# Attention of a four-layer kernel: one burst of products with v per chunk and tile, a table that deals the filling, and three moves in the heads

## The chip, the cores and the metric

The kernel runs on one core of a Trainium2 chip. Its time is device microseconds of one execution; lower is better. A core has TensorE (PE, the matrix engine, with a queue PEld for weight loads), VectorE (DVE), ScalarE (ACT), GpSimd (POOL) and SyncE (SP), which here only issues DMAs. Each engine works through its own list of instructions in order and waits on semaphores for the others.

## The reference

Four layers over 1024 tokens with 16 meta tokens ahead of them, model width 1024, batch 1, fp32. Layers 0 and 3 are sliding-window attention, layer 1 an mLSTM, layer 2 an HGRN2. Cut to what matters here:

```python
def attention_branch(u, w_in, q_gain, k_gain, sinks, w_out, valid, pos):
    q, k, v, z = _split(u @ w_in, (A_W, A_KVW, A_KVW, A_W))      # 16 heads of 64, 4 kv heads
    q = rope(rmsnorm(q), pos); k = rope(rmsnorm(k), pos)
    o = sliding_window_attention(q, k, v, sinks, valid)           # block 128: own and previous block
    return (o * silu(z)) @ w_out

def mlstm_branch(u, ...):
    q, k, v, ig, fg, og, z = _split(u @ w_in, B_SIZES)            # 8 heads, dk 128, dv 256
    qk = silu(causal_conv(concatenate([q, k]), conv_w, conv_b))
    h = mlstm_chunkwise(qh, kh, vh, log_i, log_f)                 # chunks of 128, running state
    h = rmsnorm(sigmoid(og) * h, h_gain)
    return (h * silu(z)) @ w_out

for i in range(4):
    h = h + branch_i(rmsnorm(h, norm_gain[i]), ...)
return h[:, meta:]
```

## The kernel before

The residual x lies transposed in SBUF: 8 tiles of 128 features by 1040 tokens. Tokens are cut in nine blocks, block 0 with the 16 meta tokens and blocks 1 to 8 of 128, and in three chunks of 400, 384 and 256 columns that hold blocks 0 to 3, 4 to 6, and 7 and 8. The last layer leaves the meta tokens out.

Every large product is made of three in a rounded fp32 format: weights and activations are split in a high and a low part (wh, wl and uh, ul), and high by high, high by low and low by high are added in one accumulator. Weights come by DMA on SP's queue as `wr` (128x512), ACT writes wh, VectorE wl (L188, L189). The norm of a layer's input, chunk by chunk, gives uh (ACT) and ul (VectorE). `proj` (L233) multiplies weights by 400, 384 or 256 columns of u; `proj_v` (L279) multiplies u, as weights, by 256 columns of the v weights (272 in the first mLSTM head, with the gates). For block 0 `proj_v` takes `um` (L275, u's high and low part of the meta tokens side by side), which POOL copies (L392).

The order of PE's work is written out by hand. Each layer builds lists of steps `[cost, function, prefetch]`; `weave` deals a list of filling steps (projections of later tiles, gate products) between the steps of a mixer in proportion to the costs, and the list is then emitted in that order. Weights are asked for a fixed cost ahead of their first use. The scheduler sets the order of the other engines from the order in which the steps are recorded.

An attention layer has eight tiles t of two heads hh. For each tile the mixer has units: (0,), (1,) and (2,3) in the first chunk, (4,5) and (6,) in the second, (7,8) in the third; a unit is one or two blocks. Per unit and head `S_step` makes the scores (L594, L595: q as weights, high and low part of k as columns) and the softmax on VectorE and ACT, whose last operation is ACT's L623; `T_step` transposes the result on PE (L631 for block 0, L636 for block 1, L640 otherwise) and copies it, masked, to a tile Pt; `V_step` multiplies by v (L662), 64 rows of the accumulator po for each head, and after a chunk's last unit ACT copies po out (L665). At step k of the mixer stand V_step of unit k−2, T_step of unit k−1 and S_step of unit k, and the filling is dealt by a cost of 470 for each block of the unit turned.

The second layer's head is what stands ahead of its mixer: products with v of head 0 for each chunk, gates, and the first q and k projections with their convolution (L837 to L852). Its mixer needs, per head, two rows of gate values over all 128 partitions: they are written to DRAM (L808, L809) and read back by broadcast DMAs of 520 KB each (L878, L879); L899 and L895 use them. L914 is the mixer's first product with v, its weights are wd (L188).

The lists that the change touches in the heads read, before:

```python
kv = kg0[0][:2] + vg[0][::2] + kg0[0][2:] + vg[0][1::2]      # first layer: k and v of chunk 0
head = [list(vg[0][0]), list(vg[0][1]), qg[0][0] + vg[0][2]] # second layer: v of chunks 0, 1, 2
```

Here `vg[0]` of the first layer has, for blocks 0 to 3, a first and a second half in turn; `vg[0][n]` and `qg[0][n]` of the second layer are the steps of chunk n.

Of the kernel before, what the change touches and what calls it, by code (L numbers as in the profile page):

```python
# [9 lines left out]
F32 = mybir.dt.float32  # L10
F32R = mybir.dt.float32r
# [4 lines left out]
P = 128  # L16
# [19 lines left out]
LOOKAHEAD = 12000.0  # L36
TAIL_LAG = 2000.0
PRIO = 40
ROWS, TMPS, RAWS, YS, QS = 9, 5, 2, 3, 6
XS = 13  # L40
WCOLS = 1088
GAP, BURST, PAUSE = 200.0, 1300.0, 2500.0
# [67 lines left out]
def hybrid_kernel(ctx: ExitStack, tc: tile.TileContext, ins, out, layers=(0, 1, 2, 3)):  # L110
# [309 lines left out]
    def layer_a(i, j, first, last, fin):  # L420
# [40 lines left out]
        def q_split(t):  # L461


            def step(qf, n, c0, cn):
                def fn():
                    q = qf()
                    R["q", t, n] = []
                    for hh in range(2):
                        st = R["mix"].tile([P, 400], F32R, tag="qs", name=nm("qs"), bufs=QS)
                        hs, os = slice(64 * hh, 64 * hh + 64), slice(64 - 64 * hh, 128 - 64 * hh)  # L470
                        s.copy(st[hs, :cn], q[hs])
                        v.tensor_tensor(st[os, :cn], q[hs], st[hs, :cn].bitcast(F32), op=ALU.subtract)
# [95 lines left out]
        def mixer(t):  # L568
            units = []
            for n, us in enumerate((((0,), (1,), (2, 3)), ((4, 5), (6,)), ((7, 8),))):  # L570
                if last and n == 0:
                    us = us[1:]
                for k, u in enumerate(us):
                    for hh in range(2):
                        units.append(dict(t=t, n=n, unit=u, hh=hh, first=k == 0, last=k == len(us) - 1))
            return units

        def mixers():
            def S_step(w):
# [10 lines left out]
                for u, b in enumerate(unit):  # L590
                    q0 = blk(b)[0]
                    k0, kw = (0, 16 if b == 0 else 256) if b < 2 else (q0 - P, 256)
                    qb, kb = slice(q0 - c0, q0 - c0 + nq), slice(k0, k0 + kw)
                    pe.matmul(S[:nq, u, :kw], q[:, qb], kh[:, kb], start=True, stop=False)  # L594
                    pe.matmul(S[:nq, u, :kw], q[:, qb], kl[:, kb], start=False, stop=True)  # L595
# [29 lines left out]
            def T_step(w):  # L625
                unit, Sm = w["unit"], w["Sm"]
                nu = len(unit)
                pt = psum("pt", 1).rearrange("p (u q) -> p u q", u=4)
                w["Pt"] = Pt = R["mix"].tile([P, 2, 2, P], F32, tag="Pt", name=nm("Pt"), bufs=2)
                if unit[0] == 0:  # L630
                    pe.transpose(pt[:NMETA, 0, :NMETA], Sm[:NMETA, :NMETA], ident[:NMETA, :NMETA])  # L631
                    s.copy(Pt[:NMETA, 0, 0, :NMETA], pt[:NMETA, 0, :NMETA])
                    return
                if unit[0] == 1:
                    for ki, ko in enumerate((0, NMETA)):
                        pe.transpose(pt[:, ki, :], Sm[:, ko : ko + P], ident)  # L636
                    s.copy(Pt[:, 0], pt[:, :2])
                    return
                for u in range(nu):
                    pe.transpose(pt[:, u, :], Sm[:, u, :P], ident)  # L640
                turn = R["masks"][:, M_TURN : M_TURN + 258].rearrange("p (o k c) -> p o k c", o=1, k=2)[:, :, :, :P]
                both = pt.rearrange("p u (o q) -> p u o q", o=1)[:, :nu]
                v.tensor_tensor(Pt[:, :nu], both.to_broadcast([P, nu, 2, P]), turn.to_broadcast([P, nu, 2, P]),
                                op=ALU.mult)

            def V_step(ws):
                w = ws[0]
                unit, n, t = w["unit"], w["n"], w["t"]
                nq = blk(unit[0])[1]
                if w["first"]:  # L650
                    if ("o", t) not in R:
                        R["o", t] = row()
                    R["po"] = psum("po", 1)
                po = R["po"]
                c0, cn = chunks[n]
                for u, b in enumerate(unit):
                    q0 = blk(b)[0]
                    kn, kbs = (NMETA, (0,)) if b == 0 else (P, (b - 1, b))
                    for ki, kb in enumerate(kbs):
                        for hh in range(2):  # L660
                            vc = P * (t // 4) + 64 * hh
                            pe.matmul(po[64 * hh : 64 * hh + 64, q0 - c0 : q0 - c0 + nq], V[kb][:kn, vc : vc + 64],  # L662
                                      ws[hh]["Pt"][:kn, u, ki, :nq], start=(ki == 0), stop=(ki == len(kbs) - 1))
                if w["last"]:
                    s.copy(R["o", t][:, c0 : c0 + cn], po[:, :cn])  # L665
# [5 lines left out]
            def put(seg, cost, fn, w, nu):  # L671
                step = [cost * nu, hi(lambda: fn(w)), None]
                segs[seg].append(step)
                return step

            for k in range(len(pairs) + 2):
                seg = pairs[k][0]["t"] if k < len(pairs) else 8
                v2, t1, s0 = (pairs[j] if 0 <= j < len(pairs) else None for j in (k - 2, k - 1, k))
                turned = len((t1 or v2 or s0)[0]["unit"])
                if v2:  # L680
                    put(seg, 470, V_step, v2, turned)
                elif t1:
                    segs[seg].append([470 * turned, lambda: None, None])
                for hh in range(2):
                    if t1:
                        put(seg, 110, T_step, t1[hh], len(t1[hh]["unit"]))
                    if s0:
                        step = put(seg, 236, S_step, s0[hh], len(s0[hh]["unit"]))
                        if s0[hh]["last"]:
                            order["S", s0[hh]["t"], s0[hh]["n"]] = step  # L690
# [9 lines left out]

        q0, qfin0 = qg[0]
        if first:
            kv = kg0[0][:2] + vg[0][::2] + kg0[0][2:] + vg[0][1::2]
            head = [kv, spread(kg0[1] + vg[1], kfin0[0])]
            parts = [tile_of(q0[:2], qfin0[:2]), (vg[2], [])]
        else:
            head = [kg0[0] + vg[0], spread(kg0[1], kfin0[0])]
            parts = [(vg[1][:2], []), tile_of(q0[:1], qfin0[:1]), (vg[1][2:], []), tile_of(q0[1:2], qfin0[1:2])]
# [41 lines left out]
    def layer_b(i, j, fin):  # L750
# [121 lines left out]
        def mixer(h):  # L872
            W = {}

            def start():
                R["h", h, 0], R["h", h, 1] = row(), row()
                R["rb"], R["wb"] = row(), row()
                sp.dma_start(R["rb"], R["rows_d"][0, h].partition_broadcast(P))  # L878
# [637 lines left out]
```

## Time and profile before

| | |
|---|---|
| median of 3 runs | 2586.06 us (2585.69 to 2589.89) |
| profiled execution | 2588.53 us, its span 2586.7 us |
| PE busy | 2543.5 us (98%), granted clock 0.997 on average |
| VectorE busy | 1963.4 us (76%) |
| ACT busy | 1711.5 us (66%) |
| products with v, L662 | 1056 records, 77.8 to 2533.5 us |
| DMA | 126.59 MB, 49 GB/s on average |

All rows come from one profiled execution. A row of a timeline has the start and the duration in us, the engine, the line of the kernel, the operation, out<-in, the tile, and in brackets the idle time just before it with what ended it. A matmul in this format leaves two records. Ends of matmuls are modelled, so that durations overlap; what a product costs is read from the distance of starts. Line numbers are those of the kernel before; in the changed kernel they are one to eight higher (L233 becomes L234, L279 L280, L662 L667).

### The profile page before, as it was taken

What the parts mean: (1) busy time and instruction counts of PE and PEld (TensorE: products, weight loads), DVE (VectorE), ACT (ScalarE), POOL (GpSimd) and SP (SyncE); (2) the same over time, 40 slices, a digit from 0 to 9 for tenths busy, and PEclk for the clock granted to TensorE, in tenths of its full rate; (3) what the DMA queues carried; (4) which work ended last, traced back from release to release, by engine and by line L of the source; (5) the groups of instructions that cost most, each with busy time, mean ns of one, the idle gap of its engine ahead of it and who ended that gap; (6) DMA issues with size and microseconds to landing.
All of it is one profiled execution on the core that took longest, in us unless ns stands there. A gap on an engine that the chain in (4) does not pass through costs nothing.

```text
span 2586.7 us, 55774 instructions
## 1 busy us (share of the span) xinstructions
PE 2543.5 (98%) x21009; PEld 2450.1 (95%) x21009; DVE 1963.4 (76%) x5386; ACT 1711.5 (66%) x4719; POOL 145.9 (6%) x543
## 2 busy tenths in 40 slices
PE   7999999999999999999999999999999999999999
PEld 6899899989999999999999999999999999999999
DVE  7777777886767676767777788978787978777776
ACT  7768776566565656555665757878585866868872
POOL 1100110000000000000000000101000000101000
PEclk9999999999999999999999999999999999999999
DMA  4211111011111111111111101111110111211112
GB/s 139 64 36 50 50 34 52 26 59 54 46 54 46 50 48 52 42 58 42 58 34 58 54 23 50 32 37 35 34 43 26 43 63 37 63 44 49 52 39 82
DMA packets 74191, 126.59 MB, mean 49 GB/s; under 512 B 11825, under 2 KB 26033, under 8 KB 73921
## 3 DMA queue, kind: packets, MB, share of 16 engines
q1 hardware_dynamic: 73920, 123.03, 14.8%
q8 instruction: 165, 2.70, 0.4%
q14 instruction: 106, 0.86, 0.1%
HBM read 108.14 MB, written 4.26 MB: 43 GB/s over the span
## 4 chain that ended last, share of the span: by engine, by line
PE 81%; DVE 10%; ACT 7%; issue 1%; DMA 1%; POOL 0%; SPq 0%; DVEq 0%; ACTq 0%; POOLq 0%
PE pj L233 39%; PE pj L317 16%; PE pj L279 10%; PE po L662 3%; PE pm L594 1%; PE pm L595 1%; PE pt L640 1%; PE pa L514 1%; DVE t L387 1%; PE po L914 1%; DVE ul L189 1%; PE pm L886 1%; PE pm L1192 1%; PE pj L275 1%; DVE wl L189 1%
## 5 line engine op out<-in xcount | busy, mean ns | idle before, releaser
L233 PE MATMUL pj<-uh,wh 128*128 128x384 f32 (+2 forms) x2592 | 868.3, 335 | 3.0 <-ACT uh L188 3.0
L233 PE MATMUL pj<-ul,wh 128*128 128x384 f32 (+2 forms) x2592 | 833.5, 322 | 1.8 <-DVE ul L189 1.7
L233 PE MATMUL pj<-uh,wl 128*128 128x384 f32 (+2 forms) x2592 | 831.1, 321 | 0.1
L233 PEld LDWEIGHTS pj<-uh,wh 128*128 128x128 f32 x2592 | 489.6, 189 | 22.1 <-issue 11.7
L233 PEld LDWEIGHTS pj<-ul,wh 128*128 128x128 f32 x2592 | 489.5, 189 | 6.5 <-DVE ul L189 3.6
L233 PEld LDWEIGHTS pj<-uh,wl 128*128 128x128 f32 x2592 | 489.2, 189 | 0.5 <-DVE wl L189 0.4
L189 DVE TENSOR_TENSOR wl<-wr,wh 128x512 fp32r<-128x512 f32 (+1 forms) x338 | 229.5, 685 | 54.2 <-ACT wh L188 49.3
L320 DVE TENSOR_TENSOR x<-x,pj 128x384 f32<-128x384 f32 (+2 forms) x480 | 235.6, 509 | 44.7 <-PE pj L317 42.6
L279 PE MATMUL pj<-wh,uh 128*128 128x256 f32 (+1 forms) x896 | 259.2, 289 | 0.7 <-ACT uh L188 0.7
L188 ACT CAST wh<-wr 128x512 fp32r<-128x512 f32 (+1 forms) x338 | 203.3, 613 | 83.1 <-PE pj L317 30.6
L279 PE MATMUL pj<-wh,ul 128*128 128x256 f32 (+1 forms) x896 | 253.5, 283 | 0.7 <-DVE ul L189 0.7
L317 PE MATMUL pj<-yh,wh 128*128 128x384 f32 (+2 forms) x768 | 253.0, 329 | 0.0
L279 PE MATMUL pj<-wl,uh 128*128 128x256 f32 (+1 forms) x896 | 252.7, 282 | 0.0
L317 PE MATMUL pj<-yl,wh 128*128 128x384 f32 (+2 forms) x768 | 247.4, 322 | 3.1 <-DVE yl L189 3.1
L317 PE MATMUL pj<-yh,wl 128*128 128x384 f32 (+2 forms) x768 | 246.8, 321 | 0.0
L279 PEld LDWEIGHTS pj<-wh,uh 128*128 128x128 f32 x896 | 169.4, 189 | 1.8 <-ACT uh L188 0.9
L408 ACT ACTIVATE t<-t 128x384 f32<-128x384 f32 (+2 forms) x240 | 117.7, 490 | 80.5 <-DVE t L407 77.8
L279 PEld LDWEIGHTS pj<-wh,ul 128*128 128x128 f32 x896 | 169.5, 189 | 1.2 <-DVE ul L189 1.1
L279 PEld LDWEIGHTS pj<-wl,uh 128*128 128x128 f32 x896 | 169.5, 189 | 0.7
L188 ACT CAST yh<-r 128x400 fp32r<-128x400 f32 (+2 forms) x144 | 68.6, 477 | 144.4 <-PE pj L317 134.8
L407 DVE SCALAR_TENSOR_TENSOR t<-pj,t 128x384 f32<-128x384 f32 (+2 forms) x192 | 98.8, 514 | 70.2 <-ACT t L406 66.4
L317 PEld LDWEIGHTS pj<-yl,wh 128*128 128x128 f32 x768 | 144.9, 189 | 5.0 <-DVE yl L189 4.7
(269 smaller groups left out, 5377.1 us busy)
## 6 DMA issues: line engine op xcount, KB each, us to landing
wr<-in_b_win SPq DMA_DIRECT2D x128, 256.0 KB, 2.7
wr<-in_a_win SPq DMA_DIRECT2D x80, 256.0 KB, 2.8
wr<-in_c_win SPq DMA_DIRECT2D x64, 256.0 KB, 2.7
r<-rowsd SPq DMA_DIRECT2D x16, 520.0 KB, 5.0
wr<-in_a_wout SPq DMA_DIRECT2D x32, 256.0 KB, 2.8
wr<-in_b_wout SPq DMA_DIRECT2D x32, 256.0 KB, 2.6
t<-t SPq DMA_DIRECT2D x96, 48.0 KB, 1.9
wr<-in_c_wout SPq DMA_DIRECT2D x16, 256.0 KB, 2.8
```

The costliest lines, as they stand in the source:

```text
L188: s.copy(h, src)
L189: v.tensor_tensor(l, src, h.bitcast(F32), op=ALU.subtract)
L233: pe.matmul(acc[:, :cn], a[:, k, :], b[:, k, c0 : c0 + cn], start=(k == 0 and i == 0), stop=(k == KT - 1 and i == 2))
L275: pe.matmul(acc[:48, :width], um[:, k, :], m[:, kk, :], start=(k == 0 and m is wh), stop=(k == KT - 1 and m is wl))
L279: pe.matmul(acc[:cn, :width], a[:, k, c0 : c0 + cn], m[:, kk, :], start=(k == 0 and i == 0), stop=(k == KT - 1 and i == 2))
L317: pe.matmul(acc[:, :cn], a[:, k, mc], b, start=(k == 0 and i == 0), stop=(k == 1 and i == 2))
L320: v.tensor_tensor(x[:, m, c0 : c0 + cn], x[:, m, c0 : c0 + cn], acc[:, :cn], op=ALU.add)
L387: v.scalar_tensor_tensor(u, x[:, k, cs], ngain[:, self.i, k : k + 1], self.acc[n], op0=ALU.mult, op1=ALU.mult)
L407: v.scalar_tensor_tensor(a[:, :cn], z, 0.0, a[:, :cn], op0=ALU.min, op1=ALU.subtract)
L408: s.activation(a[:, :cn], a[:, :cn], AF.Exp)
L514: pe.matmul(st[:, 2 * k : 2 * k + 2], sq[:, z : z + P], R["masks"][:, 0:P:64], start=True, stop=True)
L662: pe.matmul(po[64 * hh : 64 * hh + 64, q0 - c0 : q0 - c0 + nq], V[kb][:kn, vc : vc + 64], ws[hh]["Pt"][:kn, u, ki, :nq], start=(ki == 0), ...
```

## The change

1. `V_step` takes all units of a chunk and tile at once (`group`), after the last of them is turned, and copies the accumulator at its end.
2. So all Pt of a chunk have to live until then: block 0's has a small tile of its own (`Pt0`), single units of head 1 have `Pt1`, those of head 0 borrow a v tile, and units of two blocks keep `Pt`. The q tiles get two sizes, which makes room.
3. The filling is dealt by `SPACE`, a cost per unit, instead of 470 per block of the unit turned.
4. Block 0's scores are made over 128 columns of q instead of its 16; only the 16 are read.
5. The first layer's head makes block 0's v after that of blocks 1 to 3, in both halves.
6. The second layer's head has the first part of the q projection ahead of chunk 1's products with v instead of ahead of chunk 2's.
7. The two broadcast rows of mLSTM head 0 are asked for on POOL's queue; the other heads stay on SP's.

```diff
+SPACE = {(0,): 300.0, (1,): 470.0, (2, 3): 940.0, (4, 5): 870.0, (6,): 900.0, (7, 8): 940.0}
...
-                        st = R["mix"].tile([P, 400], F32R, tag="qs", name=nm("qs"), bufs=QS)
+                        w = 256 if n == 2 else 400
+                        st = R["mix"].tile([P, w], F32R, tag=f"qs{w}", name=nm("qs"), bufs=2 if n == 2 else 4)
...
-                    qb, kb = slice(q0 - c0, q0 - c0 + nq), slice(k0, k0 + kw)
-                    pe.matmul(S[:nq, u, :kw], q[:, qb], kh[:, kb], start=True, stop=False)
+                    qb, kb = slice(q0 - c0, q0 - c0 + P), slice(k0, k0 + kw)
+                    pe.matmul(S[:, u, :kw], q[:, qb], kh[:, kb], start=True, stop=False)
...
+                if nu == 2:
+                    Pt = R["mix"].tile([P, 512], F32, tag="Pt", name=nm("Pt"), bufs=2)
+                elif w["hh"]:
+                    Pt = R["mix"].tile([P, 256], F32, tag="Pt1", name=nm("Pt"), bufs=1)
+                else:
+                    Pt = vtile()[:, :256]
...
-            def V_step(ws):
+            def V_step(group):
...
-                for u, b in enumerate(unit):
-                    q0 = blk(b)[0]
+                for ws, u, b in ((ws, u, b) for ws in group for u, b in enumerate(ws[0]["unit"])):
+                    q0, nq = blk(b)
...
-                if w["last"]:
-                    s.copy(R["o", t][:, c0 : c0 + cn], po[:, :cn])
+                s.copy(R["o", t][:, c0 : c0 + cn], po[:, :cn])
...
-                if v2:
-                    put(seg, 470, V_step, v2, turned)
-                elif t1:
-                    segs[seg].append([470 * turned, lambda: None, None])
+                group += [v2] if v2 else []
+                space = SPACE[(t1 or v2 or s0)[0]["unit"]]
+                if v2 and v2[0]["last"]:
+                    put(seg, space, V_step, group, 1)
+                    group = []
+                elif t1 or v2:
+                    segs[seg].append([space, lambda: None, None])
...
-            kv = kg0[0][:2] + vg[0][::2] + kg0[0][2:] + vg[0][1::2]
+            kv = kg0[0][:2] + vg[0][2::2] + vg[0][:1] + kg0[0][2:] + vg[0][3::2] + vg[0][1:2]
...
-                sp.dma_start(R["rb"], R["rows_d"][0, h].partition_broadcast(P))
-                sp.dma_start(R["wb"], R["rows_d"][1, h].partition_broadcast(P))
+                queue = sp if h else g
+                queue.dma_start(R["rb"], R["rows_d"][0, h].partition_broadcast(P))
+                queue.dma_start(R["wb"], R["rows_d"][1, h].partition_broadcast(P))
...
-        head = [list(vg[0][0]), list(vg[0][1]), qg[0][0] + vg[0][2]]
+        head = [vg[0][0] + qg[0][0], list(vg[0][1]), list(vg[0][2])]
```

What the first and third point do to PE's order, in the first attention layer, tile 0, first chunk. The program's names have numbers of buffers: po is the accumulator of the products with v, Pt the turned weights of the softmax, pj the accumulator of a projection that is filling. Before, block 0's two products stand by themselves, with filling, transposes and scores behind them, and block 1's four stand by themselves again:

```order
L662 MATMUL po_946<-Pt_901,v_346 64x16
L662 MATMUL po_946<-Pt_931,v_346 64x16
L233 MATMUL pj_949<-uh,wh_736 128x400
...
L233 MATMUL pj_949<-uh,wl_737 128x400
L662 MATMUL po_946<-Pt_957,v_346 64x128
L662 MATMUL po_946<-Pt_986,v_346 64x128
L662 MATMUL po_946<-Pt_957,v_365 64x128
L662 MATMUL po_946<-Pt_986,v_365 64x128
L233 MATMUL pj_949<-uh,wh_736 128x400
```

In the changed program the chunk's products stand in one row, between the filling of a later place (v_953 is the borrowed tile):

```order
L234 MATMUL pj_1058<-uh,wl_737 128x384
L667 MATMUL po_1105<-Pt_889,v_423 64x16
L667 MATMUL po_1105<-Pt_916,v_423 64x16
L667 MATMUL po_1105<-v_953,v_423 64x128
L667 MATMUL po_1105<-Pt_982,v_423 64x128
L667 MATMUL po_1105<-v_953,v_350 64x128
L667 MATMUL po_1105<-Pt_982,v_350 64x128
L667 MATMUL po_1105<-Pt_1033,v_350 64x128
...
L667 MATMUL po_1105<-Pt_1076,v_393 64x128
L234 MATMUL pj_1058<-uh,wh_736 128x384
```

The bursts of blocks 0 and 1 have moved down to that of blocks 2 and 3; what stood around them now follows without a break.

The sixth point, on PE in the second layer's head. pj_6541 is the accumulator of block 3's v, the last of chunk 0; in the changed program the q projection (pj_6589, three of its 24 rows are shown) comes between it and chunk 1's v (pj_6645):

```order
L280 MATMUL pj_6541<-wh_6207,ul 128x272
L234 MATMUL pj_6589<-uh,wh_6376 128x400
L234 MATMUL pj_6589<-ul,wh_6376 128x400
L234 MATMUL pj_6589<-uh,wl_6377 128x400
...
L280 MATMUL pj_6645<-wh_6189,uh 128x272
```

In the program before, the row behind pj_6541 is the first of block 4's v, and the 24 rows of q stand behind chunk 1's.

The seventh point, on SP before, with the two broadcasts behind four weight loads:

```order
L808 DMA rowsd_6882<-r_6855 8x1040
L809 DMA rowsd_6882<-r_6400 8x1040
L211 DMA wr_7267<-in_b_win 128x512
L211 DMA wr_7271<-in_b_win 128x512
L211 DMA wr_7283<-in_b_win 128x512
L211 DMA wr_7287<-in_b_win 128x512
L878 DMA r_7233<-rowsd_6882 128x1040
L879 DMA r_7234<-rowsd_6882 128x1040
```

and on POOL after, between memsets of v tiles:

```order
L875 MEMSET v_7496 16x1
L876 MEMSET v_7496 16x1
L886 DMA r_7233<-rowsd_6882 128x1040
L887 DMA r_7234<-rowsd_6882 128x1040
L875 MEMSET v_7548 128x1
```

On SP the four weight loads still follow the two stores, and the loads behind them move up by two places.

More of the change, by code (lines that the diff above doesn't have):

```diff
@@ L38 @@
 PRIO = 40
-ROWS, TMPS, RAWS, YS, QS = 9, 5, 2, 3, 6
+SPACE = {(0,): 300.0, (1,): 470.0, (2, 3): 940.0, (4, 5): 870.0, (6,): 900.0, (7, 8): 940.0}
+ROWS, TMPS, RAWS, YS = 9, 5, 2, 3
 XS = 13
@@ L574, in mixer @@
                     for hh in range(2):
-                        units.append(dict(t=t, n=n, unit=u, hh=hh, first=k == 0, last=k == len(us) - 1))
+                        units.append(dict(t=t, n=n, unit=u, hh=hh, last=k == len(us) - 1))
             return units
@@ L592, in S_step @@
                     k0, kw = (0, 16 if b == 0 else 256) if b < 2 else (q0 - P, 256)
-                    qb, kb = slice(q0 - c0, q0 - c0 + nq), slice(k0, k0 + kw)
-                    pe.matmul(S[:nq, u, :kw], q[:, qb], kh[:, kb], start=True, stop=False)
-                    pe.matmul(S[:nq, u, :kw], q[:, qb], kl[:, kb], start=False, stop=True)
+                    qb, kb = slice(q0 - c0, q0 - c0 + P), slice(k0, k0 + kw)
+                    pe.matmul(S[:, u, :kw], q[:, qb], kh[:, kb], start=True, stop=False)
+                    pe.matmul(S[:, u, :kw], q[:, qb], kl[:, kb], start=False, stop=True)
                 queued = [b for b in CHUNK_BLOCKS[n] if blk(b)[0] >= c0]
@@ L628, in T_step @@
                 pt = psum("pt", 1).rearrange("p (u q) -> p u q", u=4)
-                w["Pt"] = Pt = R["mix"].tile([P, 2, 2, P], F32, tag="Pt", name=nm("Pt"), bufs=2)
                 if unit[0] == 0:
+                    w["Pt"] = Pt = R["mix"].tile([P, 1, 1, NMETA], F32, tag="Pt0", name=nm("Pt"), bufs=2)
                     pe.transpose(pt[:NMETA, 0, :NMETA], Sm[:NMETA, :NMETA], ident[:NMETA, :NMETA])
-                    s.copy(Pt[:NMETA, 0, 0, :NMETA], pt[:NMETA, 0, :NMETA])
+                    s.copy(Pt[:NMETA, 0, 0], pt[:NMETA, 0, :NMETA])
                     return
+                if nu == 2:
[4 more added lines that the diff above has]
+                    Pt = vtile()[:, :256]
+                w["Pt"] = Pt = Pt.rearrange("p (u k q) -> p u k q", k=2, q=P)
                 if unit[0] == 1:
@@ L642, in T_step @@
                 both = pt.rearrange("p u (o q) -> p u o q", o=1)[:, :nu]
-                v.tensor_tensor(Pt[:, :nu], both.to_broadcast([P, nu, 2, P]), turn.to_broadcast([P, nu, 2, P]),
+                v.tensor_tensor(Pt, both.to_broadcast([P, nu, 2, P]), turn.to_broadcast([P, nu, 2, P]),
                                 op=ALU.mult)
-            def V_step(ws):
[L647 to L654, printed above, removed]
+            def V_step(group):
+                n, t = group[0][0]["n"], group[0][0]["t"]
+                if ("o", t) not in R:
+                    R["o", t] = row()
+                po = psum("po", 1)
                 c0, cn = chunks[n]
-                for u, b in enumerate(unit):
-                    q0 = blk(b)[0]
+                for ws, u, b in ((ws, u, b) for ws in group for u, b in enumerate(ws[0]["unit"])):
+                    q0, nq = blk(b)
                     kn, kbs = (NMETA, (0,)) if b == 0 else (P, (b - 1, b))
@@ L678, in mixers @@
                 v2, t1, s0 = (pairs[j] if 0 <= j < len(pairs) else None for j in (k - 2, k - 1, k))
-                turned = len((t1 or v2 or s0)[0]["unit"])
-                if v2:
-                    put(seg, 470, V_step, v2, turned)
-                elif t1:
-                    segs[seg].append([470 * turned, lambda: None, None])
+                group += [v2] if v2 else []
+                space = SPACE[(t1 or v2 or s0)[0]["unit"]]
+                if v2 and v2[0]["last"]:
+                    put(seg, space, V_step, group, 1)
+                    group = []
+                elif t1 or v2:
+                    segs[seg].append([space, lambda: None, None])
                 for hh in range(2):
```

## The prediction

> **What bounds the kernel now.** I read the page first: the span, the busy shares and the chain that ended last.
>
> ```profile
> span 2586.7 us, 55774 instructions
> PE 2543.5 (98%) x21009; PEld 2450.1 (95%) x21009; DVE 1963.4 (76%) x5386; ACT 1711.5 (66%) x4719; POOL 145.9 (6%) x543
> PE 81%; DVE 10%; ACT 7%; issue 1%; DMA 1%; POOL 0%; SPq 0%; DVEq 0%; ACTq 0%; POOLq 0%
> ```
>
> TensorE (PE) is busy 98% of the span and is 81% of the chain; no other engine is near. The change takes no product away, so time can come from three places only: what PE loses between products of different shapes, the 2% in which it waits, and stretches at half clock. So I read the PE timeline where the shapes alternate, then the waits and the clock by stage where the order changes.
>
> **Part 1, one burst of products with v per chunk and tile.** The PE timeline of tile 0 shows a burst of the unit of block 1, and then the one of blocks 2 and 3 (start, duration, engine, line; a count is of records, and one of these products leaves two).
>
> ```profile
> 83.55 0.34 PE L233 MATMUL pj<-uh,wl 128*128 128x400 f32 x1
> 83.82 0.66 PE L662 MATMUL po<-Pt,v 128*64 128x128 f32 x8
> 84.41 0.45 PE L233 MATMUL pj<-uh,wh 128*128 128x400 f32 x1
> 84.70 0.34 PE L233 MATMUL pj<-ul,wh 128*128 128x400 f32 x1
> 84.88 0.35 PE L233 MATMUL pj<-uh,wl 128*128 128x400 f32 x1
> ```
>
> ```profile
> 89.17 0.28 PE L595 MATMUL pm<-kl,qs 128*128 128x256 f32 x1
> 89.37 1.09 PE L662 MATMUL po<-Pt,v 128*64 128x128 f32 x16
> 90.40 0.45 PE L233 MATMUL pj<-uh,wh 128*128 128x384 f32 x1
> ```
>
> Projection products follow each other every 0.18 us (84.70 to 84.88). Into the burst of four products it is 0.27, 0.09 more; the burst takes 84.41 − 83.82 = 0.59, and the first product behind it 0.29, 0.11 more. Eight products take 90.40 − 89.37 = 1.03, so four more cost 0.44, 0.11 each, and 0.59 − 0.44 = 0.15 is fixed. A burst thus costs 0.09 + 0.15 + 0.11 = 0.35 us beside its products. These two burst lengths are the only source of the 0.15; if the fixed part were nothing a burst would cost 0.20, and with 0.11 more behind the next product 0.46. I take 0.35.
>
> ```profile
> L665 ACT COPY r<-po x24: 343/457/495, 90.5 to 424.6; 128x400 f32<-128x400 f32 x8, 128x384 f32<-128x384 f32 x8, 128x256 f32<-128x256 f32 x8
> ```
>
> The copy of a finished accumulator (L665) comes 24 times in the first attention layer, 8 tiles by 3 chunks, and as often in the last. Before there is a burst per unit: six a tile in the first layer, five in the last, which has no block 0: 48 + 40 = 88. After, one per chunk: 48. So 40 go, and 40 × 0.35 = **14.0 us** (8.0 to 18.4 by the bounds). The products stay. The copy L665 followed the chunk's last burst before and does so still.
>
> **Part 2, the filling by table, and what the moved bursts covered.** Between a unit's scores and their transposes stand filling products and, until now, the previous unit's burst. The softmax on VectorE and ScalarE (ACT) has to end in that time.
>
> ```profile
> PE pt L640 <- ACT Sm L623: 4.9, 6, 2.2
> ```
>
> ```profile
> 267.90 0.28 PE L595 MATMUL pm<-kl,qs 128*128 128x256 f32 x1
> ...
> 273.64 0.68 ACT L623 ACTIVATE Sm<-Sm,s 128x128 f32<-128x128 f32 x2
> 274.19 0.52 PE L640 MATMUL pt<-ident,Sm 128*128 128x128 f32 x2
> ```
>
> The first row is a wait in the first layer (4.9 us in six times, longest 2.2). The other three are tile 4, second head of blocks 2 and 3: scores at 267.90, softmax done at 273.64 + 0.68 = 274.3, transposes due at 274.19, so 6.3 us are needed and 6.3 are there. Without the burst of block 1 (0.79 by part 1's rows) and with the table's filling some 4.7 us remain, counted in the new order: 18 products of 400 columns at 0.18 and 12 shorter operations at 0.12. That is 1.6 us of wait. Tile 0 loses 1.0 by the same count; elsewhere the table deals two blocks their 940 as before and the first units less, and some of the 4.9 us goes, which I put at 1.0. Net **−1.6 us**. The bounds: nothing is lost, or every tile of both layers loses what tile 0 does, 16.0.
>
> **Part 3, block 0's scores over 128 columns of q.** Full weights of 128 stand in for weights of 16.
>
> ```profile
> 72.66 0.17 PE L594 MATMUL pm<-r,qs 128*16 128x16 f32 x1
> 72.69 0.17 PE L595 MATMUL pm<-kl,qs 128*16 128x16 f32 x1
> 72.71 0.36 PE L233 MATMUL pj<-uh,wh 128*128 128x256 f32 x1
> 72.91 0.28 PE L233 MATMUL pj<-ul,wh 128*128 128x256 f32 x1
> ```
>
> ```profile
> 85.62 0.38 PE L640 MATMUL pt<-ident,Sm 128*128 128x128 f32 x2
> 85.75 0.42 PE L233 MATMUL pj<-uh,wh 128*128 128x384 f32 x1
> ```
>
> With 16 columns the pair takes 0.03 + 0.02, and the next product 0.20 instead of 0.12. With full weights the nearest rows are short full-width products: two transposes take 0.13. That is 0.08 more per unit, 8 tiles × 2 heads = 16 units: **−1.3 us** (0, if the 0.08 behind a change of shape goes, to −2.6). The unit's rows beyond 16 are not read.
>
> **Part 4, the second layer's head.** Before, PE goes from chunk 0's products with v straight to chunk 1's, whose normalised halves (uh on ACT, ul on VectorE) aren't ready.
>
> ```profile
> 486.80:494.20 7.40, 6.02 (x41) 5.10 (x39) 7.40 (x17) 4.35 (x12) 0.00 (x0) 1.00 0.13 41
> 494.70:498.10 3.40, 3.40 (x17) 3.40 (x17) 3.22 (x9) 2.71 (x8) 0.43 (x7) 0.50 0.07 26
> 498.10:502.10 4.00, 4.00 (x34) 4.00 (x34) 2.92 (x10) 1.67 (x7) 0.36 (x5) 1.00 0.00 0
> ```
>
> ```profile
> PE pj L279 <- DVE ul L189: 0.7, 2, 0.5
> PE pj L279 <- ACT uh L188: 0.7, 1, 0.7
> 492.78 1.02 DVE L189 TENSOR_TENSOR ul<-t,uh 128x384 fp32r<-128x384 f32 x2
> 500.26 0.75 DVE L189 TENSOR_TENSOR ul<-t,uh 128x256 fp32r<-128x256 f32 x2
> 502.15 0.35 PE L233 MATMUL pj<-uh,wh 128*128 128x400 f32 x1
> ```
>
> In windows, the number behind the times of the engines is the granted clock. At full clock 34 products take 4.0 us, 0.12 each; 41 take 4.9 and took 7.4. Two statistics products of 0.2 in all are in the stretch, so 2.3 us are lost to waiting. Right behind, at half clock, 17 took 3.4 where they need 2.0: 1.4. **Together 3.7 us.** After, the first 24 products of the q projection (0.18 × 24 = 4.4 us) stand there: chunk 0's v ends near 488.6, q at 493.0, and the last two pieces of chunk 1's ul end at 492.78 + 1.02 = 493.8, before they are wanted (18 products × 0.12 on, 495.2). Chunk 2 was covered by q (502.15); now it is wanted from 493.0 + 72 × 0.12 = 501.6 on, its last pieces 2.2 later, 503.8. They ended at 501.0; VectorE now evicts q's chunk 0 ahead of the last two, four operations (the row of L846 in part 6 has 0.62), so 503.5. It just holds.
> The Trainium skill (TensorE: Matmul & The Clock Gate, Part 1: The HAM clock gate) lets the clock fall to half after an idle window of about 3.4 us. The half-clock stretch here is that long, but no wait ahead of it is longer than 0.7 us, so by the page's rule it would not hang on these waits and would stay when they go.
>
> **Part 5, the first layer's head.** Block 0's v moves behind those of blocks 1 to 3; it needs um, which POOL makes.
>
> ```profile
> PE pj L275 <- POOL um L392: 1.1, 1, 1.1
> 19.30:22.30 3.00, 1.86 (x10) 1.00 0.58 180
> 35.30:46.00 10.70, 9.38 (x57) 1.00 0.07 19
> ```
>
> PE idles 3.00 − 1.86 = 1.1 us there, and its eight products take 2.8 where 0.9 would do: up to 1.8 are to be had. But 1.3 us of waiting come at 35 to 46 for chunk 1's norm, and an earlier PE waits there longer. I take **1.0** (0 to 1.8). The second v weights now queue on SP behind masks and constants; the DMA share is 0.58 and they are wanted 10 us later, so nothing.
>
> **Part 6, the two broadcast rows of mLSTM head 0 on POOL's queue.** They stood behind four weight loads on SP.
>
> ```profile
> 533.21 0.27 SPq L809 DMA_DIRECT2D rowsd<-r  x1
> 542.99 0.42 SPq L878 DMA_DIRECT2D r<-rowsd  x1
> DMA to landing us min/median/max: 4.8/5.3/5.8
> 549.56 0.22 DVE L899 SCALAR_TENSOR_TENSOR E<-r,bcol,caus 16x16 f32<-16x16 f32 x1
> 551.13 0.62 DVE L846 SCALAR_TENSOR_TENSOR r<-t,bcols,r 128x384 f32<-128x384 f32 x1
> 554.93 0.39 PE L914 MATMUL po<-v,wd 16*16 16x258 f32 x1 [5.77 <-ACT wd L188]
> 552.70:563.00 10.30, 8.07 (x26) 6.92 (x27) 9.47 (x30) 6.06 (x18) 0.14 (x2) 0.50 0.00 1
> ```
>
> PE waits 5.8 us for wd, then runs at half clock. The rows landed at 547.8 (542.99 + 4.8) and, the second issued 0.5 later, at 549.3, just ahead of L899, which looks like the cause. But VectorE had no idle time before L899 (its row names none): it works off the conv evictions ahead of it, like L846, and its order there is unchanged. On POOL the two rows stand behind memsets and wait only for the stores that L809 issued at 533.2; they can come some 8 us earlier, which changes nothing: **0**. Bounds: if the loads ahead of them on SP had stayed while VectorE comes 3.7 earlier, the old place would cost 549.3 − 545.9 = 3.4, which the new queue spares; the loss is case 4. Behind them on POOL stand memsets of v tiles that are wanted a block later.
>
> **Sum.** 14.0 − 1.6 − 1.3 + 3.7 + 1.0 = 15.8 us. The profiled execution took 2588.53 us for its span of 2586.7; it would take 2572.7. It lies 2.5 above the median of the runs, 2586.06; from that median the forecast is **2570.3 us**. Part 1's bounds (6.0 less, 4.4 more) and a us from the others give 2565 to 2576 as its own range.
>
> **The rivals.** (1) The wait at L914 goes too: earlier rows let the first unit's chain pass between the evictions. For: landing and use are 0.3 us apart. Against: no idle VectorE. It would give 5.8 and about 4 of the half-clock stretch (26 records in 10.3 us): 2560.5. (2) The softmax waits take half of their worst case, 8.0 instead of 1.6: 2576.7; the whole of it ends at 2584.7. For: tile 4 has no slack. Against: other units wait nowhere. (3) The wait of part 4 moves to chunk 2, as its margin of 0.3 us is thin: its 3.7 are lost, 2574.0. (4) The other side: POOL's queue delivers the two rows of 520 KB late. L899 is then late, with all of VectorE, ACT and PE behind it; each us is one us, and half as much again at half clock. The slack is 549.6 − 533.5 − 5.3 less some 3 for the stores, about 8 us; 10.5 us beyond it the 15.8 are gone, and at 24 us in all it is 2594. For: no row of this trace has such a transfer on that queue. Against: the same bytes took 5.3 us on SP. (5) The head's waits go and its half clock stays, as a state that some other thinning sets: 1.4 less, 2571.7. Against: it follows the only thinned stretch there (6.02 of 7.40).
> The Trainium skill (SBUF — State Buffer, 🔬 SBUF: two separate sides) bears on case 4: descriptors of a DMA from POOL's queue are written by GpSimd, which cannot while VectorE runs in a two-port mode; no run here shows it yet.
>
> **How the numbers follow.** Forecast 0.51, (1) 0.10, (2) 0.20, (3) 0.09, (4) 0.05, (5) 0.05. About 0.2%, 5.2 us, can be told from no change, so faster means under 2580.9: the forecast, (1), (3), (5) and somewhat over half of (2), 0.86; within it the rest of (2), 0.09; slower 0.05. The range of 2558 to 2581 takes in (1), the middle of (2) and (3), and leaves out under 2 in 10.
>
> **What would show it.** Right: 48 bursts of L667, about 0.35 us less around each that went; the wait for Sm near 6 us in the first layer; no wait of the v products for ul or uh at 488 to 504, and full clock there; the wait for wd still 5 to 6 us with half clock behind it. Wrong: a long wait of the transposes (case 2), of L899 for a DMA (4), or a PE that spends as much around 48 bursts as around 88, so that the first term is no cost of the change of shape.

## The result and the profile after

The changed kernel takes 2574.45 us (median of 6 runs, 2573.73 to 2575.38), the kernel before, run beside it, 2589.1 us; the ratio is 0.9947, with a 95% interval of 0.9936 to 0.9957. By the ratio that is 13.7 us less where 15.8 were forecast: faster, as predicted, and inside the range. (The forecast of 2570.3 us was counted from a median of three runs; 15.8 below the 2589.1 of all six is 2573.3.) The span of the profiled execution went from 2586.7 to 2573.6 us, 13.1 less.

The page of the changed kernel (span, busy shares, DMA queue of POOL, chain):

```profile
span 2573.6 us, 55775 instructions
PE 2529.4 (98%) x21009; PEld 2452.5 (95%) x21009; DVE 1957.9 (76%) x5386; ACT 1713.6 (67%) x4719; POOL 148.4 (6%) x545
q0 software_dynamic: 288, 1.07, 0.1%
PE 83%; DVE 10%; ACT 5%; DMA 1%; issue 1%; SPq 0%; POOL 0%; DVEq 0%; ACTq 0%; POOLq 0%
```

PE is as dense as before, with 14 us less to do between the same 21009 records. Where it went is read from the starts of the same products in both traces: the distance between two of them is a stage. In us, the stage before, and what each kernel adds to it or takes from it (the experiments are told below):

| stage | before | change | e1 | e2 | e3 | e4 |
|---|---|---|---|---|---|---|
| start to first scores | 72.66 | +0.57 | +1.77 | +0.58 | +0.62 | +0.04 |
| first layer, to its last product with v | 351.63 | −8.12 | −7.77 | −3.24 | −0.45 | −7.96 |
| to block 0's v of the second layer | 52.62 | 0.00 | −0.01 | +0.01 | −0.02 | +0.01 |
| second layer's head, to the first mLSTM scores | 67.45 | −3.90 | −1.84 | −3.92 | −3.81 | −3.90 |
| to the first mLSTM product with v (L914) | 10.57 | +1.97 | +0.20 | +3.56 | +0.17 | +0.02 |
| to the last layer's first scores | 1642.99 | +0.15 | −0.67 | −0.13 | −0.32 | +0.01 |
| last layer, to its last product with v | 335.58 | −3.82 | −3.64 | +0.83 | −0.17 | −3.90 |

The two attention layers give 11.9 us and the second head 3.9; the start gives nothing and the wait for wd takes 2.0 back. The burst of tile 0's first chunk on the PE timeline of the changed kernel:

```profile
89.32 0.34 PE L234 MATMUL pj<-uh,wl 128*128 128x384 f32 x1
89.59 0.29 PE L667 MATMUL po<-Pt,v 16*64 16x16 f32 x4
...
90.19 1.15 PE L667 MATMUL po<-Pt,v 128*64 128x128 f32 x17
91.27 0.45 PE L234 MATMUL pj<-uh,wh 128*128 128x384 f32 x1
91.55 0.34 PE L234 MATMUL pj<-ul,wh 128*128 128x384 f32 x1
```

One entry (0.27 from the last projection product) and one exit (0.28 to the next) stand around 14 products, where before three of each did. That it is the shape of the products that costs, and not the change of work, is borne out a little further on: the transposes, which have the 128x128 form of the projection, are entered in 0.17 us, no more than from one projection product to the next.

```profile
92.25 0.34 PE L234 MATMUL pj<-uh,wl 128*128 128x384 f32 x1
92.42 0.38 PE L649 MATMUL pt<-ident,Sm 128*128 128x128 f32 x2
```

The waits of PE in the first layer, of before (the row that the prediction shows, of 4.9 us, is left out) and of the change, and then the row of the last layer, of before and of the change:

```profile
PE pt L631 <- DVE s L608: 0.8, 1, 0.8
PE pa L514 <- ACT t L500: 0.3, 1, 0.3
```

```profile
PE pt L649 <- ACT Sm L625: 2.3, 3, 1.1
PE pt L633 <- DVE s L610: 1.0, 1, 1.0
PE po L667 <- DVE Pt L652: 0.8, 1, 0.8
PE pt L645 <- DVE Sm L611: 0.3, 1, 0.3
```

```profile
PE pt L640 <- ACT Sm L623: 0.6, 2, 0.3
```

```profile
PE pt L649 <- ACT Sm L625: 2.6, 3, 0.9
```

In the first layer the softmax waits became fewer (4.9 to 2.3 us), in the last more (0.6 to 2.6).

The second layer's head, windows at the same distance from its beginning as those quoted of before (busy times of PE, PEld, DVE, ACT, POOL, then the granted clock):

```profile
479.20:486.60 7.40, 7.40 (x49) 7.35 (x48) 7.39 (x17) 4.74 (x14) 0.00 (x0) 1.00 0.00 1
487.10:490.50 3.40, 3.40 (x29) 3.21 (x28) 3.40 (x11) 2.27 (x6) 0.00 (x0) 1.00 0.03 5
```

No wait and no half clock are left there. Then the stretch around POOL's two broadcasts, with ACT's cast of the next weights and the first mLSTM product (rows of the timeline, and the landing times of the weight loads):

```profile
521.19 0.73 POOL L886 DMA_DIRECT2D r<-rowsd  x1 [25.60 <-DMA rowsd<-r]
524.03 0.55 POOL L887 DMA_DIRECT2D r<-rowsd  x1 [2.11 <-DMA rowsd<-r]
524.27 1.97 SPq L212 DMA_DIRECT2D wr<-in_b_win  x2
528.85 0.62 ACT L189 CAST wh<-wr 128x512 fp32r<-128x512 f32 x1 [3.55 <-DMA wr<-in_b_win]
545.45 0.39 PE L922 MATMUL po<-v,wd 16*16 16x258 f32 x1 [7.74 <-ACT wd L189]
DMA to landing us min/median/max: 2.6/2.6/4.6
```

The rows are asked for at 521.2 and 524.0, some 10 us earlier than SP would (e4 below has them at 531.2), and a weight load asked for beside them takes 4.6 us instead of 2.6. ACT waits 3.55 us for it, and the wait of PE at the first mLSTM product grew from 5.77 to 7.74.

### The profile page after: what moved, and what is told of

Read it like the earlier page. It is cut to its first block, busy times and chain, and to the rows that moved or that the text cites. A ratio compares the mean times of both kernels' runs of the same rounds, so it can differ in the third digit from the quotient of the medians.

```text
span 2573.6 us, 55775 instructions
## 1 busy us (share of the span) xinstructions
PE 2529.4 (98%) x21009; PEld 2452.5 (95%) x21009; DVE 1957.9 (76%) x5386; ACT 1713.6 (67%) x4719; POOL 148.4 (6%) x545
## 4 chain that ended last, share of the span: by engine, by line
PE 83%; DVE 10%; ACT 5%; DMA 1%; issue 1%; SPq 0%; POOL 0%; DVEq 0%; ACTq 0%; POOLq 0%
PE pj L234 40%; PE pj L318 16%; PE pj L280 11%; PE po L667 3%; PE pm L596 1%; PE pm L597 1%; PE pt L649 1%; PE pa L516 1%; DVE t L388 1%; PE po L922 1%; PE pj L276 1%; DVE ul L190 1%; PE pm L894 1%; PE pm L1200 1%; PE po L924 1%
```

## The experiments

Two accounts stood against each other. Mine, from the two traces: the gain is the edges of 40 bursts and the second head; the start and POOL's queue take some back. The rivals: the filling's place, not the bursts, is what gained; the heads carry more, as the prediction had it; the rows' queue doesn't matter.

**e1, parts 1 to 4 alone.** The three moves in the heads are undone:

```diff
-            kv = kg0[0][:2] + vg[0][2::2] + vg[0][:1] + kg0[0][2:] + vg[0][3::2] + vg[0][1:2]
+            kv = kg0[0][:2] + vg[0][::2] + kg0[0][2:] + vg[0][1::2]
-                queue = sp if h else g
+                queue = sp
-        head = [vg[0][0] + qg[0][0], list(vg[0][1]), list(vg[0][2])]
+        head = [list(vg[0][0]), list(vg[0][1]), qg[0][0] + vg[0][2]]
```

> The kernel before with parts 1 to 4 of the change alone (one burst of products with v per chunk and tile, the filling dealt by the table, the tiles for it, block 0's scores over 128 columns); the three moves in the heads are undone. My account: the two attention layers carry nearly the whole gain. In the traces of before and of the change the stretch from the first scores to the last product with v went from 351.6 to 343.5 us in the first layer (8.1 less) and from 335.6 to 331.8 in the last (3.8 less); both shortenings come again within 0.5 us, and the time is 11.9 us under before. Rival: the stretches are shorter only because the heads hand over earlier (weights and normalised halves are ready sooner); then under 6 us of the 11.9 are left.

Measured: ratio 0.9956 (0.9941 to 0.9970), 11.4 us less; the two layers are 7.8 and 3.6 us shorter. The rival falls: the attention layers carry their gain by themselves. Two stages went another way than the order of the work tells. The second head, with its old order, is 1.84 shorter than before:

```profile
480.80:488.20 7.40, 6.18 (x43) 5.31 (x42) 7.39 (x17) 4.53 (x13) 0.00 (x0) 1.00 0.14 51
488.70:492.10 3.40, 3.40 (x29) 3.40 (x28) 3.21 (x9) 2.85 (x9) 0.44 (x7) 1.00 0.03 10
```

PE waits there as before (6.18 of 7.40 busy), but the clock stays at 1.00 behind it. And the start, also with the old order, is 1.77 longer, with a half-clock stretch at 22.4 to 25.8 us (granted clock 0.53 in that window) that the profile before doesn't have. So single stages move by almost 2 us with where a half-clock stretch happens to fall.

**e2, the bursts cut in two.**

```diff
-                    put(seg, space, V_step, group, 1)
+                    if len(group) > 1:
+                        put(seg, space / 2, V_step, group[:-1], 1)
+                        put(seg, space / 2, V_step, group[-1:], 1)
+                    else:
+                        put(seg, space, V_step, group, 1)
```

(V_step then takes its accumulator at a chunk's first unit and copies it at the last.)

> The changed kernel with each chunk's burst cut in two where the chunk has more than one unit: the last unit's products come one stretch of filling later, so that 80 bursts stand where the change has 48. Nothing else moves. My account: a burst costs about 0.35 us beside its products, so 32 more cost 11.2 us; the softmax waits, 7 us in the two layers, may give back up to 3 of it: 8 to 11 us slower than the changed kernel. Rival: a burst's edges are nearly free, and the change gained by where the filling stands: within 3 us of the changed kernel.

Measured: ratio 0.9984 (0.9974 to 0.9994); against the changed kernel 0.0037 of 2589, 9.6 us. The first layer is 4.88 us longer than with the change, the last 4.65, for 16 cuts each: 0.30 and 0.29 us a cut. Waits don't explain it, for they are those of the changed kernel (first layer, then last):

```profile
PE pt L649 <- ACT Sm L625: 2.6, 4, 1.1
...
PE pt L649 <- ACT Sm L625: 2.3, 3, 0.9
```

So a burst's edges cost 0.30 us, and 40 bursts fewer are worth 12.0. The same run answers whether the place of the filling gains by itself: it has the table, and 80 of the 88 bursts of before, and its two layers together are 2.4 us shorter than before, no more than the eight bursts that stay gathered are worth.

**e3, the heads alone**, on the kernel before (the edits of e1 the other way round).

> The kernel before with the three moves in the heads alone (block 0's v later in the first head, the q projection earlier in the second head, the two broadcast rows on POOL's queue). My account from the two traces: the first head loses 0.6 us (the second v weights come late), the second head gains 3.9, and the wait of the first mLSTM product for wd grows from 5.8 to 7.7: 1.3 us faster than before in all. Rival, the prediction: 1.0 + 3.7 + 0 = 4.7 us faster.

Measured: ratio 0.9997 (0.9988 to 1.0006). No difference can be told from the time, which fits 1.3 us; the interval ends at 3.1, so 4.7 lies outside it. By stages, in a profiled execution that is the fastest of ten and 3.2 us under their median, the second head gives 3.81 and the start takes 0.62, but the wait for wd did not grow this time (+0.17), although the rows are on POOL's queue. Both accounts were incomplete here.

**e4, the rows back on SP's queue** (`queue = sp`, the rest as changed).

> The changed kernel with the two broadcast rows back on SP's queue behind four weight loads. My account: VectorE's backlog, not the rows, sets the wait for wd, so the wait stays at 7.7 us within 0.7 and the time is that of the changed kernel within 1 us. Rival: the rows come late on SP now that the head is 3.9 us shorter: VectorE waits for a DMA at its first use of them, and the kernel is 2 to 5 us slower than the changed one.

Measured: ratio 0.9942 (0.9927 to 0.9957), median 2572.97; the interval overlaps the changed kernel's, so the time alone can't tell them apart; the span of the profiled execution is 2.6 us shorter.

```profile
526.54 0.62 ACT L189 CAST wh<-wr 128x512 fp32r<-128x512 f32 x1 [1.60 <-DMA wr<-in_b_win]
...
DMA to landing us min/median/max: 2.5/2.6/2.7
...
PE po L922 <- ACT wd L189: 5.8, 1, 5.8
```

Both expectations missed. Mine said that the wait for wd would stay at 7.7; it went to 5.8, and the stage is that of before. The rival said that the rows would come late; they didn't, for the weight loads ahead of them moved up with the rest. What cost the 2 us is the weight load: with the rows on SP all four land within 2.7 us, with the rows on POOL one took 4.6 in the changed kernel and 6.1 in e2, where the wait for wd is 9.3:

```profile
DMA to landing us min/median/max: 2.6/2.7/6.1
```

In e3 the loads beside POOL's rows landed in 2.7, and nothing was lost. It happens in some executions' timing, then, not in all. The same cast of ACT in e3 and in e2:

```profile
534.84 0.62 ACT L188 CAST wh<-wr 128x512 fp32r<-128x512 f32 x1 [1.70 <-DMA wr<-in_b_win]
...
535.32 0.62 ACT L189 CAST wh<-wr 128x512 fp32r<-128x512 f32 x1 [5.14 <-DMA wr<-in_b_win]
```

ACT's wait for the load is 1.60, 1.70, 3.55 and 5.14 us in e4, e3, the changed kernel and e2, and PE's wait for wd 5.8, 5.9, 7.7 and 9.3: what the load is late by comes out at PE in full.

**f1, the first head's load asked for early again** (with the rows on SP, as in f2 to f4).

```diff
+            vg[0][3][2], vg[0][1][2] = vg[0][1][2], None
             kv = kg0[0][:2] + vg[0][2::2] + vg[0][:1] + kg0[0][2:] + vg[0][3::2] + vg[0][1:2]
```

> The changed kernel with the two broadcast rows on SP's queue, and in the first head the request for the second half of the v weights hung on the first product of that half in the new order (block 1's) instead of block 0's, so that the load is asked for as early as before the change. My account: the 0.8 us of waits for wh and wl in the first head of the changed kernel go, and with the cast behind them about 1 us of restart: the first scores come at 71.2 to 72.0 us instead of 72.7 to 73.3. Rival: the waits for chunk 1's norm right behind take all of it back and the first scores stay at 72.7 or later.

Measured: ratio 0.9946 (0.9931 to 0.9961); first scores at 73.5 us, 0.8 later than in e4. The changed kernel waits for the second half of the v weights between 26 and 64 us:

```profile
PE pj L280 <- ACT wh L189: 0.5, 1, 0.5
PE pj L280 <- DVE wl L190: 0.3, 1, 0.3
```

These two rows are gone in f1, and in their place PE waits longer for the norm's sums (0.5 us in the changed kernel):

```profile
PE pa L362 <- DVE t L354: 1.5, 2, 1.0
```

The rival holds: the norm of the following chunks sets the start's end, and whatever PE gains ahead of it is waited away.

**f2, more filling ahead of the first mLSTM products.**

```diff
-                    steps += [[320, hi(lambda b=b: s1(b)), None], [PAUSE, pause, None]]
+                    steps += [[320, hi(lambda b=b: s1(b)), None], [PAUSE if h or b else 11000.0, pause, None]]
```

> The changed kernel with the rows on SP's queue, and in the mixer of mLSTM head 0 a cost of 11000 instead of 2500 for the pause between the first unit's scores and its products with v: 82 instead of 26 rows of PE stand between them. The filling dealt elsewhere in that mixer thins by some 15%. My account: the wait for wd (5.8 us) is a matter of PE arriving too early in a stretch where VectorE works off evictions; nine more filling steps of about 1 us cover it, and the half-clock stretch behind it, worth some 4 us, goes as well: 8 to 11 us faster than with the rows on SP alone. Rival: VectorE is the bound there, PE then waits at the next product for a free accumulator or for the next unit's wd: less than 3 us faster.

Measured: ratio 0.9928 (0.9911 to 0.9945), 0.0014 or 3.6 us under e4's, with intervals that overlap; the span of the profiled execution is 6.3 under e4's. From the first mLSTM scores to the last layer it is 7.0 us shorter. The first mLSTM product waits no more; what is left are waits for wd and wl at the next blocks, 2.4 us in all, and PE runs at full clock (windows of PE busy, clock):

```profile
546.11 0.29 PE L922 MATMUL po<-v,wd 16*16 16x258 f32 x1
...
PE po L922 <- ACT wd L189: 1.6, 2, 0.8
PE po L924 <- DVE wl L190: 0.8, 1, 0.8
```

```profile
540.00:552.00 12.00, 12.00 (x92) 1.00 0.21 68
552.00:562.00 10.00, 7.66 (x61) 1.00 0.00 0
```

No half-clock stretch is left in this trace between the start and the end. The gain is between the two expectations: the first wait could be filled, but of its 5.8 us 2.4 come back at the next blocks, as the rival had it. The time differs between executions: three of the four took 2566.4 to 2567.6 us at a granted clock of 0.999 to 1.000, and one 2572.0 at 0.998.

**f3, the table taken out** (470 per block, the bursts still gathered).

```diff
-SPACE = {(0,): 300.0, (1,): 470.0, (2, 3): 940.0, (4, 5): 870.0, (6,): 900.0, (7, 8): 940.0}
+SPACE = {(0,): 470.0, (1,): 470.0, (2, 3): 940.0, (4, 5): 940.0, (6,): 470.0, (7, 8): 940.0}
```

> The changed kernel with the rows on SP's queue, and the filling dealt by 470 per block of the unit turned, as before the change, in place of the table. My account: with the bursts gathered, unit (6,) has no burst of (4,5) ahead of its transposes any more and relies on the 900 of the table; with 470 its softmax is not done and PE waits 0.5 to 2 us in most of the 16 tiles: 8 to 30 us slower than with the table, as waits of the transposes for Sm. Rival: the table only smooths, within 2 us.

Measured: ratio 1.0007 (0.9998 to 1.0016): the whole gain is gone, 17 us against the same kernel with the table. The first layer is 9.7 us longer than in e4 and the last 7.5; the softmax waits of the first and the last layer:

```profile
PE pt L649 <- ACT Sm L625: 10.8, 10, 2.1
...
PE pt L649 <- ACT Sm L625: 7.8, 6, 2.3
```

So gathering the bursts takes away more cover than it saves in edges (without the table the two layers are 1.7 and 3.6 us longer than before the change), and the table gives the cover back. Some of the difference is something else: a half-clock stretch of 3.4 us, which costs at most half its length, stands in the last layer of this trace, and about 2 us of the first layer's 9.7 are in none of the waits. The prediction had costed the two together and named only the small rest.

**f4, block 0's scores over 16 columns again** (`nq` in place of `P` in the slice of q and the rows of S).

> The changed kernel with the rows on SP's queue, and block 0's scores over its 16 columns of q again. My account: 0.08 us less in each of 16 units, so that the first layer's stretch from the first scores to the last product with v is 1.3 us shorter than the 343.6 us with 128 columns. Rival: the narrow weights cost a change of shape on each side, and the stretch is as long or longer.

Measured: ratio 0.9940 (0.9925 to 0.9955); the first layer's stretch is 342.90 us against 343.67 in e4, 0.77 less. Rows of the changed kernel and of f4:

```profile
73.25 0.26 PE L597 MATMUL pm<-kl,qs 128*128 128x16 f32 x1
73.36 0.36 PE L234 MATMUL pj<-uh,wh 128*128 128x256 f32 x1
```

```profile
73.17 0.17 PE L597 MATMUL pm<-kl,qs 128*16 128x16 f32 x1
73.20 0.36 PE L234 MATMUL pj<-uh,wh 128*128 128x256 f32 x1
```

The second product of the pair takes 0.11 instead of 0.03 to the next start. The next one takes 0.20 in both, so a change of shape is paid either way. 16 × 0.08 is 1.3, and 0.8 was measured. That is not clear of chance: with 128 columns the stretch took 343.5, 343.7, 343.9 and 344.3 us in the change, e4, f1 and f2, and with 16 columns 342.9 here and 343.6 in g1. The 0.08 is shown by the rows; its worth in the layer lies somewhere between 0 and 1.3.

**g1, three edits together** (rows on SP, narrow block 0, longer pause).

> The changed kernel with three edits together: the two rows on SP's queue, block 0's scores over 16 columns, and the longer pause (11000) in mLSTM head 0's first unit. My account: the edits lie in different places and add up: 6.4 us less than with the rows on SP alone for the pause and 0.5 to 0.8 for the narrow weights, so the time is 7 us under that of the rows on SP alone and some 8.5 under the changed kernel, near 2566. Rival: the clock's state after the pause differs from run to run, and the half-clock stretch comes back (4 us of it).

Measured: ratio 0.9920 (0.9908 to 0.9933), median 2566.07 of five runs; by the ratios that is 5.7 us under e4 and 7.0 under the changed kernel, where 7 and 8.5 were expected. The longer pause gives in this trace what it gave in f2; the narrow weights show no gain here (the first layer's stretch is 343.6 us as in e4). No half-clock stretch came back in the profiled execution, but the rival holds for one run of the five: it took 2570.1 us at a granted clock of 0.998, the others 2565.2 to 2566.6 at 1.000.

**g2, and a table with 1050 for unit (6,).**

> As the kernel with the three edits, and 1050 instead of 900 in the table for unit (6,). In the trace with the rows on SP five waits of 0.87 to 1.07 us, 4.6 in all, stand ahead of the transposes of unit (6,), in tiles 0 and 4 of the first layer and three tiles of the last; counted in PE's order each of these gets about one filling step of 1 us more (3.0 to 3.6 us of cover become 3.4 to 4.7). My account: 3 to 4.5 us faster than the three edits alone. Rival: the filling comes out of units (4,5) and (2,3), whose cover falls from 5.5 to 4.5 and 5.9 to 5.4 us in four tiles, and their waits take it back: within 1.5 us.

Measured: ratio 0.9914 (0.9900 to 0.9927), median 2565.15, 0.9 under g1, less than the 3 to 4.5 us expected and within the rival's 1.5; the span of the profiled execution is 2560.9, 2.5 under g1's. The softmax waits of the last layer fell from 2.6 to 1.2 us, those of the first from 2.4 to 2.2:

```profile
span 2560.9 us, 55772 instructions
```

The intervals of g1 and g2 overlap, so only the traces tell them apart, one execution of each. g2 is 8.5 us under the changed kernel by the ratios (0.9914 against 0.9947) and has the lowest ratio of this study.

**g3, the longer pause with the rows on POOL.**

> The changed kernel, rows on POOL's queue, with the longer pause (11000). Against the same kernel with the rows on SP it tells what POOL's queue costs once PE has filling in the place. My account: the first weight load asked for behind the two stores lands late beside the two rows (4.6 us or more instead of 2.6), ACT's cast waits 3 to 5 us for it, but the longer filling covers what comes of it: within 1.5 us of the kernel with the rows on SP and the same pause. Rival: the late weight is wanted by PE's filling itself, and the kernel is 2 to 4 us slower.

Measured: ratio 0.9936 (0.9920 to 0.9951), 2.1 us over f2 by the ratios, with intervals that overlap. The weight load landed in 3.6 us, and a half-clock stretch of 3.4 us stands at that place, and another in the first layer, which has nothing to do with the queue. From the first mLSTM scores to the HGRN layer the profiled execution is 2.6 us slower than f2's, which speaks for the rival; what the traces differ by elsewhere isn't the queue's.

## Why the prediction was right, and where not

By its own terms, forecast against what the runs showed (us gained):

| part | forecast | measured | from |
|---|---|---|---|
| 1, 40 bursts fewer | 14.0 | 12.0 | e2, 0.30 a burst |
| 2, cover of the softmax | −1.6 | −0.5 | all waits of PE: 6.0 to 4.4 in the first layer, 1.1 to 3.2 in the last |
| 3, block 0's full weights | −1.3 | −0.8, not clear of chance | f4 against e4 |
| 4, second head | +3.7 | +3.9 | the stages, in four traces |
| 5, first head | +1.0 | 0 to −0.6 | the stages of e4 and of the change; f1 |
| 6, rows on POOL's queue | 0 | −2.0 | the stages of e4 and of the change |
| sum | 15.8 | 12.0 to 12.6 | the span went down by 13.1 |

Part 1 was right in mechanism and a little too dear. The step "0.59 − 0.44 = 0.15 is fixed" rested on two bursts, and "0.11 more behind the next product" on one; the cuts, 32 of them, cost 0.30 each.

Part 2 came out near by two errors that cancel. It took 6.3 us (6.4 by its own rows) as the time that tile 4's softmax needs, from the end of ACT's last operation to the scores, although ACT and VectorE also did other work in between and had the time to. In the changed kernel:

```profile
264.58 0.28 PE L597 MATMUL pm<-kl,qs 128*128 128x256 f32 x1
...
269.35 0.70 ACT L625 ACTIVATE Sm<-Sm,s 128x128 f32<-128x128 f32 x2
...
269.80 0.63 PE L649 MATMUL pt<-ident,Sm 128*128 128x128 f32 x2 [0.24 <-ACT Sm L625]
```

From these scores to the end of the softmax are 5.5 us, and PE waits 0.24 there, not 1.6. A chain that ends just in time in one order doesn't tell what it needs in another. The waits went to another unit: five of 0.9 to 1.1 us stand ahead of unit (6,), which has lost the burst of (4,5); g2 lowers these five from 4.6 us to 2.5 for that unit. So the sign that it gave, a wait for Sm near 6 us in the first layer, did not come: 2.3. And the part didn't say what f3 shows: without the table the gain is nil. That condition is the largest in the change.

Part 4 held. (Its 24 × 0.18 is 4.3 and not 4.4, which changes nothing.) But its size is partly the clock's: in e1 the old order had nearly the same waits, no half clock, and lost about 2 us less. The move is worth 2 us where the clock stays and 3.9 where it falls. So waits and half clock are not one thing, as rival 5 supposed, though e1 shows it the other way round: the waits without the half clock. In the result the rival had no weight, since with the change both are gone.

Part 5 failed in the step "they are wanted 10 us later, so nothing": PE waited 0.8 us for the load and the casts behind it. But f1 shows that this wasn't what decided; the step "an earlier PE waits there longer" should have taken all of the 1.0.

Part 6 failed in its bounds, and its sign, a wait for wd of 5 to 6 us, did not come: 7.7. It looked at the rows, whether they come early or late, and at what stands behind them on POOL's queue, and not at the loads which are under way while they run. The mechanism is that of rival 4, a late transfer on the other side, but of the weights and not of the rows. Of the rows' own use the prediction was right: VectorE's order and its lack of idle time set it, and 10 us earlier gave nothing.

Rival 1 (the wait at L914 goes too) didn't come with this change. f2 shows that more than half of the wait could be had, by filling on PE and not by earlier rows.

In the last layer 1.3 us of gain stay unexplained: 16 bursts at 0.29 less 2.1 of waits make 2.5, and 3.8 were measured.

## What to carry to other kernels

When small products of another shape are gathered, count first what they covered: here the cover lost (some 15 us, f3's two layers against e4's without the clock's share) was more than the edges saved (12), and only the filling dealt anew made it a gain. A wait of PE that lies in a stretch where a slower engine works off a backlog is filled with PE's own later work rather than cured at the operand it names, and a transfer moved earlier is judged by what else is in flight at its new place. And differences of 1 or 2 us in a stage should be checked against the granted clock in that stage before they are put down to an edit.

## What the hardware showed that was not expected

The half-clock stretches come in fixed lengths. The record of the granted clock has stretches of 3.413 us (before, in the second head; e1, at the start), 10.240 (before, e1, e3, e4, from within the wait for wd) and 13.653 (at the same place in the changed kernel, e2 and f1): one, three and four times 3.413. Nearly the same waits in the same place brought such a stretch before and none in e1. The Trainium skill (TensorE: Matmul & The Clock Gate, Part 1: The HAM clock gate) gives a free-running window of 3413 ns; the lengths agree to the nanosecond, and a window that runs free would explain why such waits count in one execution and not in another. How thin a window must be for the clock to fall, no run here shows. It need not be idle throughout: in the changed kernel the half clock begins at 539.72 us, 2.0 after the wait for wd begins (545.45 − 7.74 = 537.71), and PE was busy for 1.4 of the 3.4 us ahead of it.

Beside two broadcasts of 520 KB on POOL's queue a load of 256 KB on SP's queue took 4.6, 6.1 and 3.6 us instead of 2.6 in three of four traces; in the nine traces with the broadcasts on SP none of these loads took more than 3.0. The broadcasts themselves took 4.1 to 6.2 us on POOL's queue, and on SP's 3.6 to 6.0. The Trainium skill (SBUF — State Buffer, 🔬 SBUF: two separate sides) would have the DMA of POOL's queue late while VectorE works in its two-port mode; here it was hardly later than on SP, and the load beside it was what suffered; whether VectorE worked in that mode at the time, no view shows. Why it does so in some traces and not in e3 is open.
